# A chunked recurrence on TensorE: its triangular inverse multiplied into two operands ahead of the chain

## The chip, the cores and the metric

The kernel runs on one core of one Trainium2 chip. The metric is the device time of one execution in microseconds. TensorE is called PE, its weight loads PEld, VectorE DVE, ScalarE ACT, GpSimd POOL, and the queue that issues the DMAs SP.

## The reference

One inference step of a hybrid decoder layer, for 1024 new prompt positions and 8 sample rows: an input projection, a gated linear attention branch (GLA), an RWKV-7 branch, a gated merge of both, an output projection and a layer norm. What the change touches is the RWKV-7 branch, 16 heads of 64, whose recurrence the reference runs position by position:

```python
def _rwkv7_scan(r, w, k, v, kk, a, S0):
    def step(S, inp):
        rt, wt, kt, vt, kkt, at = inp
        sa = jnp.einsum('bhvk,bhk->bhv', S, -kkt)
        S = S * wt[:, :, None, :] + sa[..., None] * (kkt * at)[:, :, None, :] + vt[..., None] * kt[:, :, None, :]
        y = jnp.einsum('bhvk,bhk->bhv', S, rt)
        return S, y
...
p = jnp.einsum('btd,dn->btn', x, w_in)
r, kb, vb, g_b, w_lr, aa_lr = _split(pr, RWKV_SPLITS)
y, S_rwkv = _rwkv7_scan(rh, hr(w), kh, vh, kk, hr(a), S_rwkv0.astype(jnp.float32))
```

All is float32.

## The kernel before

The prompt is worked in two passes of 512 positions. In each pass the rows of the input projection (tile `proj` in PSUM, products of 128x128 weights with 256 to 512 columns, every one as three products of a high and a low part) are streamed through TensorE, and as soon as three rows of a pair of heads are there, a `pair` is started: eight pairs per pass, 16 in all, each with eight chunks of 64 positions. Beside them run the GLA heads and the gates; the up projections and the output projection come after.

Everything is written as generators that yield one operation at a time. A planner (`Order.run`) keeps an estimated time for each engine and each tile and issues, over all live generators, the operation that by its estimate can start first, with some preference by kind. So the program order of every engine is fixed when the kernel is built, and each engine runs its queue in that order. When the planner works out when an operation can start on TensorE (`start`), it adds a margin to the time at which another engine's result is ready: `SPARE`, 0.4 us for results of VectorE, ScalarE and GpSimd, and `LANDED`, 0.5, for a DMA. `self.C` is a copy that goes to ScalarE or VectorE, `self.E` an operation for VectorE or GpSimd, whichever ends first by the estimate.

A pair goes through these steps:

- `front` builds the scaled operands: `AZ` (the two left sides, 128 columns a chunk), `BK` and `GG`, the masked products within each chunk (`GG[:, x, 0]` for the chain's right side, `GG[:, x, 1]` for the output). Each chunk and head has a strictly triangular 64x64 matrix, whose unit triangular inverse is needed. Its diagonal 32x32 blocks go through DRAM (`LD`) into `L`, one block per partition, and are inverted into `X` by 31 steps on VectorE (a product into `Xt`, and an addition). The result goes back through DRAM (`XD`) into the tile `XT`, transposed, and into `X2`.
- `back` joins the two blocks of 32 into an inverse of 64: VectorE transposes the first block into `X1`, TensorE multiplies (`pA`), the result is copied (`A`), multiplied again (`pZ`), and copied into the off-diagonal part of `XT`.
- `turn` transposes `BK` on TensorE (into `bt`) and `v` (into `u`).
- `chain` runs the recurrence over the eight chunks, one pair after another: `pr` = `GG[:, x, 0]` with `u` (state and values stacked); copy to `rh`; `pu` = `XT[:, x]` with `rh`; copy the halves back to `u`; `pS` = `bt[:, x]` with `u`; and the next state from `pS`, into the next chunk's `u`. Each of the three products is 128x128 by 128 columns. After the chain, the outputs of all chunks come from two groups of products into `pY` and a `big` bank: 64x64 ones of `AZ` with the states, and 128x64 ones of `GG[:, x, 1, h]` with `u`.
- `norm` normalises, gates and writes the pair's rows.

[...] All operations are recorded by one line, L217, so that the groups in the profile are told apart by tiles. Instructions on float32 operands show as two records of TensorE each.

Of the kernel before, what the change touches and what calls it, by code (L numbers as in the profile page):

```python
# [20 lines left out]
P = 128  # L21
D = 1024
# [4 lines left out]
HT = TP // 2  # L27

PASS = [(0, HT + NS, NS, [(0, 256), (256, 264)]), (HT + NS, HT, 0, [(0, 512)])]
GH, GDK, GDV = 4, 128, 256  # L30
# [15 lines left out]
SBUF = {  # L46
    "row": ([P, HALF], 33), "wide": ([P, 2 * HT], 2), "bk": ([P, 3 * HT], 2), "gg": ([P, 4 * HT], 2), "lw": ([P, HT], 2),
    "l2s": ([P, 2 * P], 1), "pc": ([P, NCH], 3), "X": ([P, 256], 1),
    "Xt": ([P, P], 1), "L1": ([P, P], 1), "A": ([P, P], 1), "S": ([P, GDV], 2), "Sp": ([P, C], 2), "s0p": ([P, C], 2), "rh": ([P, P], 2),
    "sto": ([P, P], 1), "az": ([P, 2 * HT], 2), "bnd": ([P, 1], 3), "st": ([P, 32], 3), "part": ([P, HALF], 2), "l2p": ([P, 2 * P], 2),  # L50
    "pair": ([P, 2, HT // 32], 3), "nst": ([P, 2 * NCH], 2), "ac": ([P, HT // 4], 1),
}
# [19 lines left out]

AGE = 0.5

SPARE = 0.4
LANDED = 0.5
BIAS = 0.1
ASIDE = 0.5
# [162 lines left out]
def slow(op, us):  # L241

    op.lag = op.lag[0], op.lag[1] + us
    return op
# [11 lines left out]
class Order:  # L256
# [83 lines left out]
    def start(self, op):  # L340

        best = None
        for eng, fn, cost in op.ways:
            free, t = self.time[eng] + (SWITCH if eng == "P" and op.tiles != self.tiles else 0.0), 0.0
            for x in (*op.outs, *op.ins):
                at, by = self.ready.get(x.tensor.name, (0.0, None))
                if eng == "S" and by == "D" and x is op.out:
                    continue
                if by != eng:
                    at += HOP.get(by, 0.0) + (SPARE if eng == "P" and by in ("V", "A", "G") else LANDED if by == "D" else 0.0)  # L350
                elif eng != "P" and x is not op.out:
                    at += 0.13
                t = max(t, at)
            t = max(t, *(self.read.get(x.tensor.name, 0.0) for x in op.outs))
            if eng in op.port:
                free = max(free, self.port["G" if eng == "V" else "V"])
            late, t = free - t, max(t, free)
            if eng in "VA" and self.held(eng, op):
                cost += HOLD
            end = t + cost  # L360
            if len(op.ways) > 1:
                end += BIAS if eng == "V" and "A" in op.ways[0][0] else ASIDE if eng == "G" and "G" in op.port else 0.0
            if best is None or end < best[0]:
                best = end, t
                op.eng, op.fn, op.cost, op.late = eng, fn, cost, max(0.0, late)
        return best[1]
# [56 lines left out]
class Kern(Order):  # L423
# [711 lines left out]
    def front(self, c, p, st, d):  # L1135
# [85 lines left out]
        for q in range(4):  # L1221
            yield slow(self.S.dma_start(L_[NU * q:NU * q + NU], LD.rearrange("n c s t -> (n c) (s t)")), 1.0)
        tm = yield from self.get("Xt")
        for j in range(31):
            w, ni = 31 - j, j // 4 + 1
            tv = tm[:, :ni * w].rearrange("p (s t) -> p s t", t=w)
            yield V.tensor_mul(tv, X[:, 0:ni, j:j + 1].to_broadcast([P, ni, w]),
                               L[:, j:j + 1, j + 1:].to_broadcast([P, ni, w]))
            yield V.tensor_add(X[:, 0:ni, j + 1:], X[:, 0:ni, j + 1:], tv)
        self.free(tm)  # L1230
        XT = (yield from self.get("XT")).rearrange("p (c h t) -> p c h t", c=NCH, h=2)
        XD = self.dr.tile([4 * NCH, 32, 32], F32, name=f"XD{c.i}{p}")
        for q in range(4):
            yield slow(self.S.dma_start(XD.rearrange("u (i g) t -> g u i t", g=4)[q], X[NU * q:NU * q + NU]), 0.5)
        self.free(X_)

        L1 = (yield from self.get("L1")).rearrange("p (x t) -> p x t", t=32)
        X2 = (yield from self.get("X2")).rearrange("p (g t) -> p g t", t=P)
        H = NCH // 2
        for h in range(2):  # L1240
            for n in range(2):
                g = 2 * h + n
                yield slow(self.S.dma_start(L1[32 * g:32 * g + 32], GG[64 * h:64 * h + 32, H * n:H * n + H, 0, h, 32:64]), -0.5)
        for q in range(2):
            b = slice(32 * q, 32 * q + 32)
            for h in range(2):
                n = 2 * q + h
                yield self.S.dma_start(XT[HS[h]][b, :, h, b], XD[n * NCH:(n + 1) * NCH].rearrange("c s t -> s c t"))

        for x in range(H):  # L1250
            b = slice(32 * x, 32 * x + 32)
            yield self.S.dma_start(X2[b, :, b], XD[2 * NCH + x::H].rearrange("g s t -> s g t"))
        d.AZ, d.BK, d.G, d.XT, d.v, d.bonus, d.pc, d.L, d.L1, d.X2 = AZ, BK, GG, XT, st[2], st[1], pc, L_, L1, X2

    def back(self, d):
        GG, XT = d.G, d.XT

        H = NCH // 2
        X1 = (yield from self.get("X1")).rearrange("p (x t) -> p x t", t=P)
        q = [slice(32 * n, 32 * n + 32) for n in range(4)]  # L1260
        for h in range(2):
            for n in range(2):
                g = 2 * h + n
                yield self.V.transpose(X1[q[g], :, q[g]], XT[q[2 * h], H * n:H * n + H, h, 0:32])
        pA = yield from self.bank("big", [P, P])
        yield together([self.P.matmul(pA[q[x]], d.L1[:, x], X1[:, x], start=True, stop=True) for x in range(H)])
        A_ = yield from self.get("A")
        yield self.C.copy(A_, pA)
        self.free(pA, X1, d.L1)
        pZ = yield from self.bank("big", [P, H, 32])  # L1270
        yield together([self.P.matmul(pZ[q[g]], A_[:, q[g]], d.X2[:, g], start=True, stop=True) for g in range(4)])
        for h in range(2):
            for n in range(2):
                yield self.C.copy(XT[q[2 * h], H * n:H * n + H, h, 32:64], pZ[q[2 * h + n]])

        for h, hs in enumerate(HS):
            yield self.C.copy(GG[hs, :, 0, h], d.AZ[hs, :, 0])
        self.free(pZ, A_, d.X2)

    def turn(self, d):  # L1280

        bt = d.BK.rearrange("p c t -> p (c t)")[:, :2 * HT].rearrange("p (c h k) -> p c h k", c=NCH, h=2)
        pt = yield from self.get("big", 2)
        yield together([self.tr(pt[h][:, x * C:x * C + C], d.BK[hs, x, h * C:h * C + P])
                        for x in range(NCH) for h, hs in enumerate(HS)])
        for h in range(2):
            yield self.C.copy(bt[:, :, h], pt[h].rearrange("p (c k) -> p c k", k=C))
        self.free(*pt)
        d.bt = bt.rearrange("p c h k -> p c (h k)")
        d.u = d.L.rearrange("p (c h v) -> p c h v", c=NCH, h=2)  # L1290
        pt = yield from self.bank("big", [P, 4, P])
        for n in range(4):
            yield self.tr(pt[:, n], d.v[:, n * P:(n + 1) * P])
        self.free(d.v)
        for h in range(2):
            for n, hs in enumerate(HS):
                yield self.C.copy(d.u[HS[1 - h], n::2, h], pt[hs, :, h * C:h * C + C])
        self.free(pt)

    def chain(self, c, p, d):  # L1300
        A, V = self.A, self.V
        AZ, BK, GG, XT, pc = d.AZ, d.BK, d.G, d.XT, d.pc
        u_, bt_ = d.u, d.bt

        for h, hs in enumerate(HS):
# [7 lines left out]
        for x in range(NCH):  # L1313
            u = u_[:, x]
            pr = yield from self.bank("pch", [P, 2, C])
            yield self.P.matmul(pr, GG[:, x, 0], u, start=True, stop=True)
            rh = yield from self.get("rh")
            yield V.tensor_copy(rh, pr)
            self.free(pr)
            s0p = None  # L1320
            if x >= first:
                for h, hs in enumerate(HS):
                    yield A.copy(ss[hs, x], u[hs, h])
                s0p = yield from self.get("s0p")
                yield A.activation(s0p, ss[:, x], AF.Copy, scale=pc[:, x:x + 1])
            pu = yield from self.bank("pch", [P, 2, C])
            yield self.P.matmul(pu, XT[:, x], rh, start=True, stop=True)
            self.free(rh)
            for h, hs in enumerate(HS):
                yield self.C.copy(u[hs, h], pu[hs, h])  # L1330
            self.free(pu)
            pS = yield from self.bank("pch", [P, 2, C])
            yield self.P.matmul(pS, bt_[:, x], u, start=True, stop=True)
            for h, hs in enumerate(HS):
                un = u_[hs, x + 1, h] if x + 1 < NCH else S[hs]
                if s0p is None:
                    yield V.tensor_scalar(un, pS[hs, h], pc[hs, x:x + 1], None, ALU.mult)
                else:
                    yield V.scalar_tensor_tensor(un, pS[hs, h], pc[hs, x:x + 1], s0p[hs], ALU.mult, ALU.add)
            self.free(pS, *([] if s0p is None else [s0p]))  # L1340
# [10 lines left out]
            yield V.scalar_tensor_tensor(y[:, :, h], mean[:, :, h].unsqueeze(2).to_broadcast([P, H, C]), -1.0 / RN, pY[h],  # L1351
                                         ALU.mult, ALU.add)
        self.free(*pY, ss_)
        self.free(AZ, BK, u_, GG, XT, pc)
        if c.i:
            self.spawn(self.state(p, S), "state")
        else:
# [482 lines left out]
```

## Time and profile before

| | |
|---|---|
| median of 3 runs | 1489.15 us (1487.49 to 1490.96) |
| the profiled execution | 1487.92 us, span 1486.1 us |
| granted TensorE clock | 0.996 |
| busy, share of the span | PE 98%, PEld 85%, DVE 80%, ACT 58%, POOL 8% |
| DMA | 318.96 MB, 66.8% of 16 engines' span |
| the chain's products (`pch`) | from 135.2 us to 1262.1 us of the span |

In the rows of a profile, "out<-in" names the tiles without their numbers, then come the shapes and the count; "busy, mean" is a group's time and one record's; what stands behind the second bar is the idle time of the engine ahead of it and what ended it. In a timeline a row has its start, its length, the engine, the operation and the count of merged records. TensorE's records overlap each other, so that distances from start to start tell more than lengths.

### The profile page before, as it was taken

The numbers are of one execution on the slowest core, as the hardware profiler recorded it, in microseconds if no ns is written. First come the engines' busy times: TensorE is split into PE (matmuls) and PEld (weight loads), VectorE is DVE, ScalarE is ACT, GpSimd is POOL, SyncE is SP. The second block draws the span as 40 slices with busy tenths as digits, with TensorE's granted clock in tenths as the row PEclk, the third lists the DMA queues.
The fourth block names the chain that finished last, engine by engine and source line by source line (L and its number), as shares of the span: only waits on it lengthen the run. The fifth ranks groups of instructions, "written<-read, shape, count | busy, mean of one in ns | idle before, by whom it ended". The sixth has DMA issues, their size and how long they took to land. (4 is left out here: it accounts for less than half of the span.)

```text
span 1486.1 us, 31563 instructions
## 1 busy us (share of the span) xinstructions
PE 1449.8 (98%) x11158; PEld 1260.4 (85%) x11158; DVE 1194.8 (80%) x3255; ACT 857.7 (58%) x2196; POOL 113.6 (8%) x208
## 2 busy tenths in 40 slices
PE   9999999999999999999999999999999999999997
PEld 6998999899989998787777777878787898988786
DVE  6697889888998899879878989898877866755665
ACT  5666776676767776665754555474547645544210
POOL 1001010201010102000101020111001000000000
PEclk9999999999999999999999999999999999999999
DMA  8886786678676877566566556656564766888432
GB/s 299 273 285 202 250 296 214 226 253 295 202 258 211 294 229 258 170 224 188 160 198 179 155 190 191 192 154 188 174 189 138 229 210 221 295 293 271 139 107 85
DMA packets 211258, 318.96 MB, mean 215 GB/s; under 512 B 91811, under 2 KB 107180, under 8 KB 211100
## 3 DMA queue, kind: packets, MB, share of 16 engines
q1 hardware_dynamic: 211100, 316.93, 66.8%
q8 instruction: 89, 1.46, 0.4%
q14 instruction: 69, 0.57, 0.1%
HBM read 197.19 MB, written 118.61 MB: 212 GB/s over the span
## 5 line engine op out<-in xcount | busy, mean ns | idle before, releaser
L217 PE MATMUL proj<-xs,wpart 128*128 128x264 f32 (+2 forms) x5640 | 1017.7, 327 | 1.4 <-DVE row L217 0.8
L217 PEld LDWEIGHTS proj<-xs,wpart 128*128 128x128 f32 x5640 | 808.5, 189 | 80.3 <-issue 9.9
L217 ACT CAST wpart<-wraw 128x512 fp32r<-128x512 f32 x210 | 130.2, 623 | 103.5 <-PE proj L217 49.6
L217 DVE TENSOR_TENSOR row<-row 128x512 f32<-128x512 f32 (+7 forms) x321 | 166.3, 524 | 12.4 <-ACT row L217 5.6
L217 DVE TENSOR_TENSOR wpart<-wraw,wpart 128x512 fp32r<-128x512 f32 x207 | 145.2, 702 | 32.3 <-ACT wpart L217 31.4
L217 ACT ACTIVATE row<-row 128x512 f32<-128x512 f32 (+5 forms) x213 | 128.8, 610 | 14.4 <-DMA row<-sg 6.5
L217 POOL TENSOR_TENSOR row<-row 128x512 f32<-128x512 f32 (+5 forms) x64 | 72.7, 1143 | 746.3 <-DVE row L217 396.4
L217 DVE TENSOR_TENSOR Xt<-X,wide 128x60 f32<-128x60 f32 (+24 forms) x496 | 104.8, 211 | 11.7 <-DMA wide<-LD 1.8
L217 DVE TENSOR_TENSOR X<-X,Xt 128x60 f32<-128x60 f32 (+24 forms) x496 | 105.4, 213 | 10.0
L217 ACT ACTIVATE row<-proj,omu 128x256 f32<-128x256 f32 (+1 forms) x99 | 54.0, 546 | 93.5 <-PE proj L217 93.3
L217 PE MATMUL big<-xs,wpart 128*128 128x256 f32 (+2 forms) x576 | 101.7, 332 | 0.0
L217 PEld LDWEIGHTS big<-xs,wpart 128*128 128x128 f32 x576 | 87.7, 194 | 9.7 <-issue 0.2
L217 DVE SCALAR_TENSOR_TENSOR wide<-pch,pc,s0p 64x64 f32<-64x64 f32 x208 | 58.7, 282 | 32.9 <-PE pch L217 28.0
L217 ACT COPY row<-wide 64x64 f32<-64x64 f32 x240 | 57.9, 241 | 40.2 <-DVE wide L217 34.7
L401 ACT ACT_TABLE_LOAD x62 | 79.5, 1283 | 1.1
L217 DVE SCALAR_TENSOR_TENSOR row<-proj,pv,row 128x255 f32<-128x255 f32 (+1 forms) x99 | 56.3, 569 | 22.4 <-ACT tail L217 13.7
L217 PE MATMUL big<-row 128*32 128x32 f32 (+4 forms) x936 | 65.3, 241 | 1.4 <-ACT row L217 1.4
L217 ACT COPY row<-big 128x128 f32<-128x128 f32 (+6 forms) x134 | 38.7, 318 | 42.2 <-PE big L217 36.7
L217 ACT COPY wide<-pch 64x64 f32<-64x64 f32 x159 | 32.8, 206 | 47.0 <-PE pch L217 45.1
L217 ACT ACTIVATE row<-proj 128x128 f32<-128x128 f32 (+4 forms) x136 | 36.9, 324 | 37.4 <-PE proj L217 37.0
L217 PE MATMUL pch<-wide,gg 128*128 128x128 f32 x256 | 51.6, 283 | 5.5 <-DVE wide L217 4.7
L217 PEld LDWEIGHTS pch<-wide,gg 128*128 128x128 f32 x256 | 42.3, 189 | 16.1 <-PE proj L217 4.7
(249 smaller groups left out, 1992.6 us busy)
## 6 DMA issues: line engine op xcount, KB each, us to landing
w<-wpart SPq DMA_DIRECT2D x146, 512.0 KB
wpart<-w SPq DMA_DIRECT2D x146, 512.0 KB
wraw<-w_in SPq DMA_DIRECT2D x146, 256.0 KB
wide<-LD SPq DMA_DIRECT2D x64, 128.0 KB
wraw<-w_up_gla SPq DMA_DIRECT2D x32, 256.0 KB
wraw<-w_up_rwkv SPq DMA_DIRECT2D x32, 256.0 KB
sg<-row SPq DMA_DIRECT2D x16, 260.0 KB
row<-sg SPq DMA_DIRECT2D x16, 260.0 KB
```

What stands on the lines that cost most here:

```text
L217: ways.append((eng, lambda call=call: call(out, *args, **kw), price(eng, name, out, args, ins)))
L401: self.nc.scalar.preload_act_table_set(self.table)
```

## The change

The inverse is no longer applied in the chain to every chunk's right side. It is multiplied into `bt` and into the output matrix `GG[:, x, 1]` beforehand, in `turn`: with P the inverse, `bt`'·(P·r) becomes (P'-multiplied `bt`)'·r, and the same for the output. In the chain, `pr` is copied to `u` directly, and the product `pu` and the tile `rh` are gone: two products per chunk instead of three. To multiply in this order, the inverse is needed untransposed (`XI`, half as wide as `XT`): the solve runs over columns from the last to the first and reads `L` by columns, `X1` is loaded by DMA where `X2` was, and `back` transposes the other block and copies the quarters of `pA` into `X2`. The margin `SPARE` becomes one per engine: 0.6 for VectorE and GpSimd, 0.2 for ScalarE.

```diff
-SPARE = 0.4
+SPARE = {"V": 0.6, "G": 0.6, "A": 0.2}
...
-                    at += HOP.get(by, 0.0) + (SPARE if eng == "P" and by in ("V", "A", "G") else LANDED if by == "D" else 0.0)
+                    at += HOP.get(by, 0.0) + (SPARE[by] if eng == "P" and by in SPARE else LANDED if by == "D" else 0.0)
... (front)
-        for j in range(31):
-            w, ni = 31 - j, j // 4 + 1
-            tv = tm[:, :ni * w].rearrange("p (s t) -> p s t", t=w)
-            yield V.tensor_mul(tv, X[:, 0:ni, j:j + 1].to_broadcast([P, ni, w]),
-                               L[:, j:j + 1, j + 1:].to_broadcast([P, ni, w]))
-            yield V.tensor_add(X[:, 0:ni, j + 1:], X[:, 0:ni, j + 1:], tv)
+        LT = L.rearrange("p s t -> p t s")
+        for j in range(31, 0, -1):
+            i, ni = j // 4, 8 - j // 4
+            tv = tm[:, :ni * j].rearrange("p (s t) -> p s t", t=j)
+            yield V.tensor_mul(tv, X[:, i:, j:j + 1].to_broadcast([P, ni, j]),
+                               LT[:, j:j + 1, :j].to_broadcast([P, ni, j]))
+            yield V.tensor_add(X[:, i:, :j], X[:, i:, :j], tv)
...
-        XT = (yield from self.get("XT")).rearrange("p (c h t) -> p c h t", c=NCH, h=2)
+        XI = (yield from self.get("XT"))[:, :HT].rearrange("p (c t) -> p c t", c=NCH)
...
+        for h in range(2):
+            for n in range(2):
+                b, o = slice(64 * h + 32 * n, 64 * h + 32 * n + 32), h * NCH + H * n
+                yield self.S.dma_start(X1[b, :, b], XD[o:o + H].rearrange("c s t -> s c t"))
         for q in range(2):
             b = slice(32 * q, 32 * q + 32)
             for h in range(2):
                 n = 2 * q + h
-                yield self.S.dma_start(XT[HS[h]][b, :, h, b], XD[n * NCH:(n + 1) * NCH].rearrange("c s t -> s c t"))
+                yield self.S.dma_start(XI[HS[h]][b, :, b], XD[n * NCH:(n + 1) * NCH].rearrange("c s t -> s c t"))
-        for x in range(H):
-            b = slice(32 * x, 32 * x + 32)
-            yield self.S.dma_start(X2[b, :, b], XD[2 * NCH + x::H].rearrange("g s t -> s g t"))
... (back)
-                yield self.V.transpose(X1[q[g], :, q[g]], XT[q[2 * h], H * n:H * n + H, h, 0:32])
         pA = yield from self.bank("big", [P, P])
-        yield together([self.P.matmul(pA[q[x]], d.L1[:, x], X1[:, x], start=True, stop=True) for x in range(H)])
-        A_ = yield from self.get("A")
-        yield self.C.copy(A_, pA)
+        yield together([self.P.matmul(pA[q[x]], d.L1[:, x], d.X1[:, x], start=True, stop=True) for x in range(H)])
+        for x in range(H):
+            for h in range(2):
+                yield self.V.transpose(A_[q[x], 2 * h:2 * h + 2], XI[q[2 * h + 1], x::H, 32:64])
+        for x in range(H):
+            yield self.C.copy(X2[q[x], :, x], pA[q[x]].rearrange("p (g t) -> p g t", t=32))
... (turn)
+        pf = yield from self.get("big", 2)
+        pf = [y.rearrange("p (x k t) -> p x k t", k=2, t=C) for y in pf]
+        yield together([self.P.matmul(pf[h][HS[x % 2], x // 2, k], d.XI[hs, x], (bt[hs, x, h], d.G[hs, x, 1, h])[k], start=True, stop=True)
+                        for i in range(0, NCH, 2) for k in range(2) for x in (i, i + 1) for h, hs in enumerate(HS)], 0.5)
+        for k in range(2):
+            for h, hs in enumerate(HS):
+                for n in range(2):
+                    yield self.C.copy(d.G[hs, n::2, 1, h] if k else bt[hs, n::2, h], pf[h][HS[n], :, k])
+        self.free(*pf, d.XI)
... (chain)
             yield self.P.matmul(pr, GG[:, x, 0], u, start=True, stop=True)
-            rh = yield from self.get("rh")
-            yield V.tensor_copy(rh, pr)
-            self.free(pr)
...
-            pu = yield from self.bank("pch", [P, 2, C])
-            yield self.P.matmul(pu, XT[:, x], rh, start=True, stop=True)
-            self.free(rh)
             for h, hs in enumerate(HS):
-                yield self.C.copy(u[hs, h], pu[hs, h])
-            self.free(pu)
+                yield self.C.copy(u[hs, h], pr[hs, h])
+            self.free(pr)
```

More of the change, by code (lines that the diff above doesn't have):

```diff
@@ L48 @@
     "l2s": ([P, 2 * P], 1), "pc": ([P, NCH], 3), "X": ([P, 256], 1),
-    "Xt": ([P, P], 1), "L1": ([P, P], 1), "A": ([P, P], 1), "S": ([P, GDV], 2), "Sp": ([P, C], 2), "s0p": ([P, C], 2), "rh": ([P, P], 2),
+    "Xt": ([P, P], 1), "L1": ([P, P], 1), "A": ([P, P], 1), "S": ([P, GDV], 2), "Sp": ([P, C], 2), "s0p": ([P, C], 2),
     "sto": ([P, P], 1), "az": ([P, 2 * HT], 2), "bnd": ([P, 1], 3), "st": ([P, 32], 3), "part": ([P, HALF], 2), "l2p": ([P, 2 * P], 2),
@@ L1237, in front @@
         L1 = (yield from self.get("L1")).rearrange("p (x t) -> p x t", t=32)
-        X2 = (yield from self.get("X2")).rearrange("p (g t) -> p g t", t=P)
+        X1 = (yield from self.get("X1")).rearrange("p (x t) -> p x t", t=P)
         H = NCH // 2
@@ L1247, in front @@
                 n = 2 * q + h
-                yield self.S.dma_start(XT[HS[h]][b, :, h, b], XD[n * NCH:(n + 1) * NCH].rearrange("c s t -> s c t"))
-        for x in range(H):
-            b = slice(32 * x, 32 * x + 32)
-            yield self.S.dma_start(X2[b, :, b], XD[2 * NCH + x::H].rearrange("g s t -> s g t"))
[L1253 to L1260, printed above, removed]
+                yield self.S.dma_start(XI[HS[h]][b, :, b], XD[n * NCH:(n + 1) * NCH].rearrange("c s t -> s c t"))
@@ new lines, in front, with back @@
+        d.AZ, d.BK, d.G, d.XI, d.v, d.bonus, d.pc, d.L, d.L1, d.X1 = AZ, BK, GG, XI, st[2], st[1], pc, L_, L1, X1
+    def back(self, d):
+        GG, XI = d.G, d.XI
+        H = NCH // 2
+        q = [slice(32 * n, 32 * n + 32) for n in range(4)]
+        pA = yield from self.bank("big", [P, P])
+        yield together([self.P.matmul(pA[q[x]], d.L1[:, x], d.X1[:, x], start=True, stop=True) for x in range(H)])
+        A_ = (yield from self.get("A")).rearrange("p (g t) -> p g t", t=32)
+        for x in range(H):
+            for h in range(2):
+                yield self.V.transpose(A_[q[x], 2 * h:2 * h + 2], XI[q[2 * h + 1], x::H, 32:64])
+        X2 = (yield from self.get("X2")).rearrange("p (g x t) -> p g x t", g=4, t=32)
+        for x in range(H):
+            yield self.C.copy(X2[q[x], :, x], pA[q[x]].rearrange("p (g t) -> p g t", t=32))
+        self.free(pA, d.X1, d.L1)
+        pZ = yield from self.bank("big", [P, H, 32])
+        yield together([self.P.matmul(pZ[q[g]], A_[:, g], X2[:, g].rearrange("p x t -> p (x t)"), start=True, stop=True) for g in range(4)])
@@ L1261, in back @@
         for h in range(2):
             for n in range(2):
-                g = 2 * h + n
-                yield self.V.transpose(X1[q[g], :, q[g]], XT[q[2 * h], H * n:H * n + H, h, 0:32])
-        pA = yield from self.bank("big", [P, P])
-        yield together([self.P.matmul(pA[q[x]], d.L1[:, x], X1[:, x], start=True, stop=True) for x in range(H)])
-        A_ = yield from self.get("A")
-        yield self.C.copy(A_, pA)
-        self.free(pA, X1, d.L1)
-        pZ = yield from self.bank("big", [P, H, 32])
@@ L1271, in back @@
[L1271 to L1274, printed above, removed]
+                yield self.C.copy(XI[q[2 * h + 1], H * n:H * n + H, 0:32], pZ[q[2 * h + n]])
         for h, hs in enumerate(HS):
             yield self.C.copy(GG[hs, :, 0, h], d.AZ[hs, :, 0])
-        self.free(pZ, A_, d.X2)
+        self.free(pZ, A_, X2)
@@ L1298, in turn @@
         self.free(pt)
+        pf = yield from self.get("big", 2)
[7 more added lines that the diff above has]
+        self.free(*pf, d.XI)
     def chain(self, c, p, d):
         A, V = self.A, self.V
-        AZ, BK, GG, XT, pc = d.AZ, d.BK, d.G, d.XT, d.pc
+        AZ, BK, GG, pc = d.AZ, d.BK, d.G, d.pc
         u_, bt_ = d.u, d.bt
@@ L1353, in chain @@
         self.free(*pY, ss_)
-        self.free(AZ, BK, u_, GG, XT, pc)
+        self.free(AZ, BK, u_, GG, pc)
         if c.i:
```

## The prediction

> **What bounds the kernel now.** I read the page's busy table first, then its slices, then PE's own waits, and then single stretches of PE's timeline.
>
> ```profile
> span 1486.1 us, 31563 instructions
> PE 1449.8 (98%) x11158; PEld 1260.4 (85%) x11158; DVE 1194.8 (80%) x3255; ACT 857.7 (58%) x2196; POOL 113.6 (8%) x208
> PE   9999999999999999999999999999999999999997
> DVE  6697889888998899879878989898877866755665
> ```
>
> TensorE has work in every slice; the other engines have room, DVE least of all (eight or nine tenths through the middle). So a microsecond is gained by taking occupancy from PE's in-order queue or by taking out a wait at its head. What the waits come to, by PE's rows of the view of waits (engine, line, releaser: us in total, times, longest):
>
> ```profile
> PE pch L217 <- DVE wide L217: 6.0, 9, 1.7
> PE pch L217 <- DVE rh L217: 4.1, 4, 1.8
> PE big L217 <- DVE part L217: 3.0, 5, 0.9
> PE big L217 <- DVE row L217: 2.2, 3, 1.3
> PE big L217 <- DVE X L217: 1.7, 1, 1.7
> PE big L217 <- ACT row L217: 1.4, 2, 1.0
> PE big L217 <- DMA X<-XD: 1.2, 1, 1.2
> PE big L217 <- DVE S L217: 1.1, 3, 0.5
> PE pch L217 <- ACT wide L217: 1.0, 3, 0.5
> ```
>
> These are 21.7 us of the 36.3 us (1486.1 less 1449.8) in which PE is idle. The recurrence is not the bound: its links are issued between projection products, and PE is late for a link only in a few places. So the sum is one of PE occupancy, with a small term for waits.
>
> **Removed: one 128x128 product per chunk (`pu` from `XT` and `rh`), 2 passes x 8 pairs x 8 chunks = 128.** The page's group view says this, but the matmuls overlap there, so I take the price from the timeline, as what the product displaces among projection products:
>
> ```profile
> L217 PE MATMUL pch<-rh,XT 128*128 128x128 f32 x256 | 51.1, 281 | 4.1 <-DVE rh L217 4.1
> 603.54 0.38 PE L217 MATMUL pch<-rh,XT 128*128 128x128 f32 x2
> 603.68 1.63 PE L217 MATMUL proj<-xs,wpart 128*128 128x512 f32 x6
> 605.15 0.38 PE L217 MATMUL pch<-wide,bk 128*128 128x128 f32 x2
> ...
> 1298.22 16.82 PE L217 MATMUL big<-xs,wpart 128*128 128x512 f32 x72
> 1314.88 11.27 PE L217 MATMUL proj<-xs,wpart 128*128 128x512 f32 x48
> ```
>
> An undisturbed 128x512 product costs (1314.88 - 1298.22)/72 = 0.2314 us from start to start. From the `rh` product to the next link lie 605.15 - 603.54 = 1.61 us with six of those (1.39) in them: the f32 product, two records, costs 0.22 us. 128 x 0.22 = **28.2 us off PE**. Its busy time, 51.1 us, would be 0.40 each; I don't take it, because the tail of a record lies under the next one's head.
>
> **The wait for `rh` goes with it: 4.1 us** (row above), as the product that waited is gone. Late next is the same chunk's `u`: the copies from `pr` now come right behind `pr`, where they came behind `pu`; their wait (ACT wide, 1.0 us) is kept as it is. Nothing is queued behind a new wait in the chain: it has one hop through DVE and one link fewer.
>
> **Added in `turn`: 32 products of 64x64x64 per pair, 512 in all.** The profile has the same shape with the same order of quarters in the output block `pY` (row half by head, column half by chunk parity):
>
> ```profile
> 670.64 0.48 PE L217 MATMUL proj<-xs,wpart 128*128 128x512 f32 x1
> 671.05 0.27 PE L217 MATMUL pY<-row,az 64*64 64x64 f32 x1
> ...
> 671.16 0.22 PE L217 MATMUL pY<-row,az 64*64 64x64 f32 x1
> ...
> 671.45 0.22 PE L217 MATMUL pY<-row,az 64*64 64x64 f32 x1
> ...
> 671.51 0.22 PE L217 MATMUL big<-row,az 64*64 64x64 f32 x1
> 671.66 0.69 PE L217 MATMUL pY<-wide,gg 128*64 128x64 f32 x16
> ...
> 672.75 18.11 PE L217 MATMUL proj<-xs,wpart 128*128 128x512 f32 x77
> 690.78 0.41 PE L217 MATMUL big<-row 128*32 128x32 f32 x25
> ```
>
> From 671.16 to 671.45 five steps of four records pass, 0.058 us each; a step is two products (f32 is two records). 32 products are 16 steps: 0.93 us. The first step is 0.05 longer (671.05 to 671.16). Leaving for another shape takes 0.15 from the last record (671.51 to 671.66), 0.09 over a step. Entering from a projection takes 0.41 - 0.23 = 0.18. Returning costs something on the first projection: 690.78 - 672.75 = 18.03 against 77 x 0.2314 = 17.82, so at most 0.2 for this and the next change of shape; I take half, 0.1. A block is 0.93 + 0.05 + 0.09 + 0.18 + 0.10 = 1.35 us, 16 of them **21.6 us onto PE**. Bounds: 1.07 (17.1 in all) where entry and exit are shared with the transposes that `turn` has just issued; 1.45 (23.2) with the full 0.2. I take 1.35, as the nearest block in the trace stands among projections.
>
> **Copies and transposes on DVE and ACT.** Their groups, by shape:
>
> ```profile
> L217 DVE COPY rh<-pch 128x128 f32<-128x128 f32 x128 | 37.0, 289 | 17.5 <-PE pch L217 14.7
> L217 DVE COPY wide<-big 64x256 f32<-64x256 f32 x31 | 13.1, 423 | 4.7 <-PE big L217 4.2
> L217 ACT COPY wide<-big 64x256 f32<-64x256 f32 x33 | 12.1, 367 | 6.0 <-DVE wide L217 5.5
> L217 DVE STREAM_TRANSPOSE X<-XT 32x128 f32<-32x128 f32 x64 | 19.2, 300 | 4.9 <-DMA XT<-XD 4.3
> L217 ACT COPY XT<-big 32x128 f32<-32x128 f32 x43 | 11.0, 256 | 7.3 <-PE big L217 6.7
> ```
>
> Gone: 128 `rh` copies, 37.0 us of DVE. New: 8 copies of 64x256 out of `pf` per pair, 128 x 0.367 to 0.423 = 47 to 54 us over both engines. `back` has 128 half-sized transposes for 64 (each between half of 0.300 and all of it: 0 to 19 us more on DVE; nearer all, as fixed costs rule at this size, so 11) and four quarter copies for the one `A` copy (three more of 0.256, 12 us, mostly on ACT). Halved between the engines, DVE ends about even (-37 + 25 + 11 + 3) and ACT gains about 33 us on 857.7 of 1486.1. The cover is PE's projection work, which fills the queue while a pair is in `back` and `turn`; I cost it at nothing. Without the cover, the eight copies on two engines, 4 x 0.4 = 1.6 us per pair, would be waited for: 26 us.
>
> **The rest, in one go.** The solve counts down instead of up; its pairs of instructions keep their number and sizes (31 to 1 columns by 1 to 8 blocks), and only L is read down a column. The DMAs keep their number and shape: four loads into `X1` for the four into `X2`, ahead of the four into `XI` on SP's queue, so `XI` comes four issues later and the first product in `back` now waits for `X1`'s landing in place of DVE's transposes (the 1.7 us wait `<- DVE X` becomes one for a DMA like the 1.2 us one): nothing, between -1.7 and +1.2. `XT`'s buffer is free before the chain instead of after it, and the new need of two `big` banks lasts some 3 us per pair.
>
> **Margins.** The order is planned with 0.6 us in hand for DVE and POOL results at PE (0.4 before) and 0.2 for ACT's. The 20 DVE waits in the rows that remain (9 + 5 + 3 + 3) lose at most 0.2 us each, 4.0 us; the five ACT waits gain 0.2 each, 1.0 us, and others can appear. I take **-2.0**, between -4.0 and a loss that I price as a rival.
>
> **Sum**: -28.2 + 21.6 - 4.1 - 2.0 = -12.7 us. The profiled execution took 1487.92 us (span 1486.1 and 1.8 around it), so 1475.2; it lay 1.2 us under the median of 1489.15, to which I add it: **1476 us**. What counts as no change is 0.2%, 3 us.
>
> **The rivals.**
>
> *Slower: ACT's results come too late at PE.* With 0.2 us less in hand, each product fed by ACT may stall PE 0.2 us. There are some 430 such places:
>
> ```profile
> L217 ACT CAST wpart<-wraw 128x512 fp32r<-128x512 f32 x210 | 130.2, 623 | 103.5 <-PE proj L217 49.6
> L217 ACT COPY wide<-pch 64x64 f32<-64x64 f32 x159 | 32.8, 206 | 47.0 <-PE pch L217 45.1
> ```
>
> and 64 casts of `xs`. Without the -2.0 the sum is -10.7; it turns into a loss over 3 us when 13.7 us are stalled, 69 places, one in six. At one in four, 108 x 0.2 = 21.6, the time is 1489 - 10.7 + 21.6 = 1500. Against it: ACT stands still 103.5 us ahead of the casts alone, and PE has only five such waits in the rows above. 0.12.
>
> *No change: the gain goes into new waits.* `pf` must be copied before the chain starts, and DVE is the fullest of the helpers. If half of the 26 us of copies shows at PE, 1476 + 13 = 1489. For it: DVE's eights and nines; against it: 21.7 us of waits in 1486. 0.09.
>
> *More gained: the shorter chain also ends the waits on `wide`, and blocks share their switches.* 6.0 us of `<- DVE wide` and 21.6 - 17.1 = 4.5 more, with the full 4.0 of the margins: 1476 - 6.0 - 4.5 = 1465.5, and with the overlap of the first two taken as none, some 1464. For it: `turn` issues its transposes just ahead; against it: `u` still comes over the same DVE hop from `pS`. 0.14.
>
> *The solve slows down.* In column order an element lies 128 bytes from the next. If each paid its time twice, then by the groups kept apart by shape (for `pc`, the view of its tile: min/median/max)
>
> ```profile
> L217 DVE TENSOR_TENSOR Xt<-X,wide 128x76 f32<-128x76 f32 x16 | 3.9, 244 | 0.3
> L217 DVE TENSOR_TENSOR Xt<-X,wide 128x24 f32<-128x24 f32 x16 | 3.0, 186 | 0.4
> L217 DVE COPY pc<-row x15: 156/164/664, 55.2 to 1144.2; 128x8 f32<-128x8 f32 x15
> L217 DVE TENSOR_SCALAR nkk<-pv 128x8 f32<-128x8 f32 x1 | 0.2, 165 | 0.0
> ```
>
> (244 - 186)/52 = 1.1 ns an element, 1560 elements per pair and 16 pairs, 27 us of DVE; all of it at PE would make 1503. Against it: `pc` takes eight elements 260 bytes apart in a median 164 ns, and `nkk` eight adjacent ones in 165. 0.03. [...]
>
> *Four quarters don't run side by side in `pf`*: 16 steps become 32, 0.93 us more a block, +15: 1491. `pY` speaks against it, 0.02.
>
> **How the numbers follow.** 0.60 for 1476 (its own range 1468 to 1484, from blocks of 1.07 to 1.45 us and margins of -4 to +2), 0.14, 0.09, 0.12, 0.03, 0.02 for the others in the order more, none, ACT, solve, quarters. Faster by over 0.2%: 0.60 + 0.14 and a little of "none", 0.76; within: 0.10; slower: 0.14. From 1463 to 1491 lies all but the two slow ends and the lower part of "more", under 0.2.
>
> **What the changed profile would show.** 256 `pch` product records in each of two groups, none from `rh`; a group of 1024 64x64 records into `big` with 0.058 us steps; PE's waits at 15 to 20 us with fewer `<- DVE` and a few more `<- ACT`; DVE's busy time within 15 us of 1194.8 and ACT's some 30 higher; the `Xt<-X,wide` means as they were. I am wrong if the blocks cost over 1.8 us, or if PE's idle time grows past 45 us.

## The result, and the profile after

| | before | after |
|---|---|---|
| median | 1488.32 us (1485.46 to 1490.96, 4 runs) | 1501.61 us (1498.94 to 1504.05, 4 runs) |
| profiled execution, span | 1486.1 us | 1502.3 us |
| granted TensorE clock | 0.996 | 0.988 |

The ratio is 1.0091, with a 95% interval of 1.0068 to 1.0114: the kernel became slower by 13 us, where 1476 us was forecast. The page of the changed kernel, its busy table and two rows of its slices:

```profile
span 1502.3 us, 33264 instructions
PE 1452.7 (97%) x11926; PEld 1254.1 (83%) x11926; DVE 1212.1 (81%) x3207; ACT 894.2 (60%) x2335; POOL 117.4 (8%) x223
PE   9999999999999999999999999999999989999997
PEclk9999999999999999999999999999999999999999
```

PE is idle for 1502.3 - 1452.7 = 49.6 us, 13.3 more than before, and its busy time has not fallen. The slices hide why: nine tenths of the clock and full clock print the same digit. The mean granted clock shows it. If PE's pace follows the clock, as it does in the block of products below (1.09 us at full clock, 2.11 at half), (1 - 0.988) x 1502.3 = 18.0 us were lost to a reduced clock, against (1 - 0.996) x 1486.1 = 5.9 before, 12.1 more. Nearly all of that lies within PE's busy time (some 2 us of it in each kernel fall behind the last product). What PE does at full clock fell from 1449.8 - 5.9 = 1443.9 to 1452.7 - 18.0 = 1434.7. So the 16.2 us between the two profiles are 13.3 of idle time, 12.1 of clock, and -9.2 of work. (The clock is given to three digits; each clock term is good to some 0.8 us.) This split belongs to one execution, the slowest of the four: the other three of the changed kernel had granted clocks of 0.992, 0.989 and 0.994, which by the same sum are 12.0, 16.5 and 9.0 us lost.

At this place the forecast has 28.2 off and 21.6 on, -6.6 us. The -9.2 us bears that out only roughly, because PE's busy time holds more than the products' own work: two runs below, `n1_order` and `r6_rows`, have the same products in the same order and granted clocks of 0.996 and 0.995, and yet 5.3 us between their busy times:

```profile
PE 1441.8 (97%) x11926; PEld 1246.8 (84%) x11926; DVE 1217.4 (82%) x3247; ACT 876.1 (59%) x2287; POOL 121.9 (8%) x227
PE 1436.5 (97%) x11926; PEld 1247.9 (84%) x11926; DVE 1202.1 (81%) x3247; ACT 873.4 (59%) x2287; POOL 122.4 (8%) x227
```

What the new products cost is better read from PE's timeline. One block of them:

```profile
656.16 1.08 PE L217 MATMUL proj<-xs,wpart 128*128 128x512 f32 x4
657.18 0.34 PE L217 MATMUL big<-bk,XT 64*64 64x64 f32 x8
657.34 0.30 PE L217 MATMUL big<-gg,XT 64*64 64x64 f32 x8
657.46 0.30 PE L217 MATMUL big<-bk,XT 64*64 64x64 f32 x8
...
658.04 0.30 PE L217 MATMUL big<-gg,XT 64*64 64x64 f32 x8
658.27 1.66 PE L217 MATMUL proj<-xs,wpart 128*128 128x512 f32 x6
```

From 657.34 to 657.46 eight records (four products, one for each head and chunk parity) pass in 0.12 us, so a step of four takes 0.058 as in `pY`. The block lasts from 657.18 to 658.27, 1.09 us, with 0.10 of entry in front of it (1.02 for four projections of 0.2314). With the slow first projection behind it that is the 1.35 us of the forecast, within 0.1. In the trace 15 of the 16 blocks last 1.09 us from their first product to the next one behind them; the last, at half clock, lasts 2.11.

PE's waits, in the view of waits of the changed kernel:

```profile
PE big L217 <- DMA X<-XD: 6.0, 3, 3.0
PE big L217 <- DMA XT<-XD: 5.6, 7, 1.2
PE pch L217 <- DVE wide L217: 4.7, 10, 0.9
PE big L217 <- DVE part L217: 3.7, 3, 2.3
PE big L217 <- ACT X L217: 3.3, 1, 3.3
PE big L217 <- DVE X L217: 2.7, 2, 1.8
PE proj L217 <- DMA wpart<-w: 2.3, 1, 2.3
```

The wait for `rh` is gone, as said. At the top stand 11.6 us for the inverse's blocks coming out of `XD`; before, this was 1.2. Ten times PE stood in front of the first product of `back` until the loads had landed; the profile puts these down to `X` or `XT`, which are issued one behind the other. The longest of these on PE's timeline:

```profile
487.83 2.41 PE L217 MATMUL proj<-xs,wpart 128*128 128x264 f32 x19
493.25 0.47 PE L217 MATMUL big<-X,L 128*32 128x128 f32 x8 [3.01 <-DMA X<-XD]
493.65 4.36 PE L217 MATMUL proj<-xs,wpart 128*128 128x256 f32 x22
```

And what such a wait does to the clock, by stretches of the changed kernel (length; busy time of PE, PEld, DVE, ACT, POOL with counts; granted clock; DMA):

```profile
262.00:264.80 2.80, 0.52 (x4) 0.34 (x3) 2.80 (x6) 1.36 (x3) 1.89 (x6) 1.00 0.61 143
264.80:268.20 3.40, 3.40 (x20) 2.86 (x21) 2.88 (x7) 1.44 (x3) 0.00 (x0) 0.50 0.67 176
299.50:302.40 2.90, 1.13 (x9) 0.92 (x9) 2.74 (x8) 0.00 (x0) 1.10 (x2) 0.99 0.53 215
302.40:305.80 3.40, 3.40 (x16) 3.12 (x15) 3.01 (x11) 2.04 (x10) 0.00 (x0) 0.50 0.07 27
490.50:493.50 3.00, 0.25 (x8) 0.19 (x8) 1.77 (x3) 1.35 (x3) 0.86 (x4) 1.00 0.61 148
493.50:496.90 3.40, 3.40 (x23) 3.25 (x16) 2.62 (x10) 0.71 (x4) 0.00 (x0) 0.50 0.94 312
497.00:520.00 23.00, 23.00 (x272) 21.10 (x271) 17.02 (x33) 17.77 (x55) 3.83 (x7) 1.00 0.76 261
```

Behind 3.00 us in which PE is busy for 0.25, the clock is at half for 3.4 us. If PE does half as much in them, as the block of 2.11 us against 1.09 says, the wait of 3.0 us costs some 1.7 more, an estimate (half of 3.4). The first pair of stretches shows the same behind a wait for `part`, the second behind 1.8 us of idle time (2.90 less 1.13). The kernel before has this too, behind several waits close together near its end (2.3 us of idle time in 4.30), but not behind 1.8 us of idle time at 781 us:

```profile
781.00:784.00 3.00, 1.17 (x6) 0.69 (x6) 2.97 (x8) 0.61 (x1) 0.00 (x0) 1.00 0.32 119
784.00:787.00 3.00, 3.00 (x16) 2.24 (x14) 2.87 (x8) 1.45 (x4) 0.00 (x0) 1.00 0.29 71
1232.00:1236.30 4.30, 2.01 (x14) 1.60 (x13) 4.24 (x10) 3.67 (x9) 0.00 (x0) 1.00 0.58 223
1236.30:1243.00 6.70, 6.18 (x30) 5.98 (x29) 2.54 (x7) 3.04 (x8) 0.00 (x0) 0.50 0.66 197
```

So the length of a wait does not decide alone; what decides beside it, no run shows. In the trace's clock records all half-clock stretches of the changed kernel begin whole multiples of 3.41 us apart: those at 264.8, 302.4, 493.5, 592.5 and 988.4 us lie 11, 56, 29 and 116 such steps from one to the next. That 1.8 to 3.0 us of standing still were enough at these places is measured; that they are enough everywhere is not, by the 1.8 us at 781.

Last, the solve. All its products and those of 8 elements in the kernel before, then the same groups as in the forecast in the changed kernel:

```profile
L217 DVE TENSOR_TENSOR Xt<-X,wide 128x60 f32<-128x60 f32 (+24 forms) x496 | 104.8, 211 | 11.7 <-DMA wide<-LD 1.8
L217 DVE TENSOR_TENSOR Xt<-X,wide 128x8 f32<-128x8 f32 x16 | 2.6, 162 | 0.2
...
L217 DVE TENSOR_TENSOR Xt<-X,wide 128x60 f32<-128x60 f32 (+24 forms) x496 | 127.1, 256 | 14.4 <-DMA wide<-LD 4.2
L217 DVE TENSOR_TENSOR Xt<-X,wide 128x76 f32<-128x76 f32 x16 | 4.7, 294 | 0.4
L217 DVE TENSOR_TENSOR Xt<-X,wide 128x24 f32<-128x24 f32 x16 | 2.9, 182 | 0.3
L217 DVE TENSOR_TENSOR Xt<-X,wide 128x8 f32<-128x8 f32 x16 | 2.6, 164 | 0.3
```

127.1 us where the page before has 104.8: 22 us more on VectorE, 1.4 us per pair. At 8 and at 24 elements nothing is lost (164 ns after 162, 182 after 186), but these take one and three elements of a column of L, each for eight blocks; between 24 and 76 (19 of a column for four blocks) each further element costs (294 - 182)/52 = 2.2 ns where it cost (244 - 186)/52 = 1.1. The planner's price for these products is by their size alone, so it takes every result of the solve, and what follows it on VectorE, as ready earlier than it is.

### The profile page after: what moved, and what is told of

The parts are those of the page before. It is cut to its first block, busy times and chain, and to the rows that moved or that the text cites. A ratio compares the mean times of both kernels' runs of the same rounds, so it can differ in the third digit from the quotient of the medians.

```text
span 1502.3 us, 33264 instructions
## 1 busy us (share of the span) xinstructions
PE 1452.7 (97%) x11926; PEld 1254.1 (83%) x11926; DVE 1212.1 (81%) x3207; ACT 894.2 (60%) x2335; POOL 117.4 (8%) x223
## 4 chain that ended last, share of the span: by engine, by line
PE 68%; DVE 18%; DMA 6%; SPq 3%; issue 3%; ACT 2%; POOL 0%; POOLq 0%; DVEq 0%; ACTq 0%
PE proj L217 40%; PE big L217 21%; DVE row L217 6%; SPq L217 3%; PE pY L217 3%; PE pch L217 3%; DVE Xt L217 3%; DVE X L217 3%; DVE wpart L217 1%; ACT row L217 1%; DMA wpart<-w 1%; DVE wide L217 1%; DMA wide<-LD 1%; DVE pair L217 1%; DMA X<-XD 1%
## 5 line engine op out<-in xcount | busy, mean ns | idle before, releaser
L217 DVE TENSOR_TENSOR row<-row 128x512 f32<-128x512 f32 (+8 forms) x328 | 170.1, 526 | 8.0 <-ACT row L217 3.2
L217 DVE TENSOR_TENSOR wpart<-wraw,wpart 128x512 fp32r<-128x512 f32 x199 | 138.5, 698 | 30.6 <-ACT wpart L217 29.3
L217 DVE TENSOR_TENSOR Xt<-X,wide 128x60 f32<-128x60 f32 (+24 forms) x496 | 127.1, 256 | 14.4 <-DMA wide<-LD 4.2
L217 DVE TENSOR_TENSOR X<-X,Xt 128x60 f32<-128x60 f32 (+24 forms) x496 | 110.0, 222 | 9.8
L217 POOL TENSOR_TENSOR row<-row 128x512 f32<-128x512 f32 (+5 forms) x57 | 62.7, 1103 | 638.8 <-DVE row L217 257.9
L217 PE MATMUL big<-xs,wpart 128*128 128x512 f32 (+2 forms) x576 | 100.2, 330 | 0.3 <-DVE xs L217 0.2
L217 PEld LDWEIGHTS big<-xs,wpart 128*128 128x128 f32 x576 | 86.4, 191 | 10.8 <-DVE xs L217 0.8
L217 ACT COPY row<-wide 64x64 f32<-64x64 f32 x240 | 58.0, 242 | 60.3 <-DVE wide L217 51.1
L217 ACT COPY row<-big 128x128 f32<-128x128 f32 (+6 forms) x157 | 43.3, 301 | 64.1 <-PE big L217 43.2
L217 ACT CAST xs<-row 128x520 fp32r<-128x520 f32 (+1 forms) x64 | 38.5, 623 | 29.4 <-PE big L217 11.7
```

The costliest lines, as they stand in the source:

```text
L217: ways.append((eng, lambda call=call: call(out, *args, **kw), price(eng, name, out, args, ins)))
```

## The experiments

Two theories stood first: that the inverse comes too late (by the column reads and by X1's landing), and that the margins put PE ahead of its results. "Bias" below is a constant of the planner, `ASIDE`, that counts against giving an operation to GpSimd; changing it makes another order of the same work, with some operations on other engines.

**Margins undone; margins alone.** `SPARE` at 0.4 for all in the changed kernel, and the new dictionary in the kernel before.

> The changed kernel with the margin of before (0.4 us for each engine). Theory 1 (late inverse: reading L by columns makes the solve longer than the planner's price, so PE stands at the first product of back until X1 has landed, and long stalls halve PE's clock): the margin is no part of it, the time stays at 1496 to 1506 us, with over 8 us of PE waits for DMAs out of XD. Theory 2 (the margins put PE ahead of its results): it falls to 1480 or less.

> The kernel before with the new margins alone (0.6 us for VectorE and GpSimd, 0.2 for ScalarE). Theory 1: within 4 us of before, as nothing of the inverse changes. Theory 2: 1495 or more, with over 6 us of PE waits on ScalarE where before had 3.5.

The first took 1497.36 us (ratio to before 1.0066, 1.0046 to 1.0085), the second 1486.15 (0.9997, 0.9982 to 1.0012). The margins alone change nothing that can be measured; the forecast took -2.0. Theory 2 fell with these two: in the kernel before, PE's waits for ScalarE were 3.6 us with the new margins and 3.5 without. In the changed kernel they are 6.9 us in seven places, and 3.4 with the margins undone; that is far from the 21.6 us of the forecast's slower rival, but the 4 us by which the first run is below the changed kernel are not told apart from another order (see below). Theory 1 missed one of its signs in that run: the waits for `XD` were 6.7 us, under the 8 expected.

**L read along its rows.** The same instructions in the same order on every engine, with other addresses; the inverse is then not the right one.

```diff
-                               LT[:, j:j + 1, :j].to_broadcast([P, ni, j]))
+                               L[:, j:j + 1, :j].to_broadcast([P, ni, j]))
```

> The changed kernel, but the solve reads L along its rows (contiguous) where it should read columns, so the inverse is not the right one; the order of all instructions is the same as in the changed kernel. Theory 1: the products into Xt fall back from 127 us to about 105, PE's waits for DMAs out of XD from 11.6 us to under 6, fewer clock halvings, and the time to 1488 or less. Theory 2: 1498 to 1504 as the changed kernel. A third theory (the copies of pf load DVE and ACT): also 1498 to 1504.

1488.15 us (1.0008, 0.9995 to 1.0022): 13.5 us less than the changed kernel. The group `Xt` is back:

```profile
L217 DVE TENSOR_TENSOR Xt<-X,wide 128x60 f32<-128x60 f32 (+24 forms) x496 | 108.0, 218 | 14.2 <-DMA wide<-LD 3.9 <-issue 0.2
```

But theory 1 was wrong about the way: the waits for `XD` should have fallen under 6 us, and its waits are

```profile
PE big L217 <- DMA XT<-XD: 4.3, 6, 1.1
PE big L217 <- DMA X<-XD: 3.5, 2, 2.8
```

7.8. What fell was PE's idle time, from 49.6 to 43.0 us, and the stretches at half clock, from seven (30.7 us) to three (13.7), which is 8.5 us of the gain. So what the column reads cost does not come through the waits for `XD` alone. The third theory, that the copies of `pf` cost the time, expected 1498 or more and fell here too.

**Both prices of the planner mended; X1's landing alone.** `e5_priced` adds 0.7 ns per element to the price of the column-read products and 1.5 us to the landing time of X1's loads; `e4_x1_late` only the latter:

```diff
-                yield self.S.dma_start(X1[b, :, b], XD[o:o + H].rearrange("c s t -> s c t"))
+                yield slow(self.S.dma_start(X1[b, :, b], XD[o:o + H].rearrange("c s t -> s c t")), 1.5)
```

> The changed kernel with two prices of the planner mended and nothing else: 0.7 ns more per element for the solve's column-read products, and 1.5 us later landing for the loads of X1. Theory 1: PE waits for DMAs out of XD fall under 3 us, PE's clock is halved in at most four places, and the time comes to 1476 to 1488. Theory 2: no change beyond the noise of the order, 1495 or more.

> The changed kernel with X1's loads planned 1.5 us later, the solve's price left as it is. If the wait at X1's landing was the larger part of what the priced version gained: 1490 to 1494, with no PE wait for DMAs out of XD. If it was the price of the column reads (all of VectorE's results were planned too early): 1496 or more, although those waits are gone.

1491.62 us (1.0040, 1.0028 to 1.0053), and 1483.50 (0.9970, 0.9955 to 0.9986). In the second, the waits for `XD` are down from 11.6 to 1.1 us:

```profile
PE big L217 <- DMA X<-XD: 0.6, 1, 0.6
PE big L217 <- DMA XT<-XD: 0.5, 1, 0.5
```

Both came out of their ranges: the priced one worse than expected, with no `XD` wait left, and the half-mended one better than it. A planner with the truer price lost to one with the falser: the first sign that the order as such moves the time by as much as the causes do.

**Both causes away; another way round; another order.** `e6_rows_x1_late` joins the two edits above. `e7_copied` lets ScalarE turn L within each partition, and keeps the later landing of X1:

```diff
+        two = yield from self.rows(2, 512)
+        LT = [x.rearrange("p (t s) -> p t s", s=32) for x in two]
+        for q in range(2):
+            yield A.copy(LT[q], L[:, :, 16 * q:16 * q + 16].rearrange("p s t -> p t s"))
```

> The solve reading L along rows (so the inverse is not the right one) and X1's loads planned 1.5 us later. If column reads and X1's landing are two causes that add up, and they are all that stood between the changed kernel and the sum of its products: PE idle 33 to 38 us, at most three halvings of the clock, and 1474 to 1482 us. If something else costs the rest (the copies of pf, or the order itself): 1484 to 1490.

> The changed kernel computing the right thing with the column reads taken from VectorE: ScalarE copies L transposed within each partition into two free row buffers, and the solve reads that along rows; X1's loads planned 1.5 us later. ScalarE gets 16 x 2 copies of 512 elements, some 20 to 35 us. If the column reads and X1's landing were the causes: 1476 to 1486. If the order as such or the copies of pf are: 1488 or more.

> [...] Each theory that names a cause expects 1496 to 1507; a time under 1492 would say that the slowdown was an accident of this one order.

1471.52 us (0.9890, 0.9870 to 0.9909), 1497.61 (1.0065, 1.0034 to 1.0096) and 1489.29 (1.0009, 0.9995 to 1.0023). The first is below its range, and below the sum that the forecast made; its partner in the same order is `e4_x1_late`, 12.0 us above it. The second removes the column reads from VectorE (`Xt` at a median of 212 ns) and is slow all the same, with 10.1 us of waits for `part` in ten places and five stretches at half clock. It is no clean trial of the column reads, as the solve now waits for ScalarE's copies:

```profile
L217 DVE TENSOR_TENSOR Xt<-X,row 128x60 f32<-128x60 f32 (+24 forms) x496 | 110.5, 223 | 29.9 <-ACT row L217 19.5
```

The third, with `ASIDE` at 0.6 in place of 0.5, moved 12 us by an edit that means nothing, to under the 1492 that was to speak for an accident of one order. From here on, a single order proved nothing, and each version was taken in three.

> The changed kernel in a third order (bias against GpSimd 0.4 in place of 0.5; 0.6 gave 1489). If the changed kernel's 1501.6 is one end of a spread of orders: anything from 1485 to 1504, most likely 1488 to 1498. PE waits of 8 us or more for DMAs out of XD in any case.

> The same third order's bias, with X1's loads planned 1.5 us later. If the wait at X1's landing costs by itself, whatever the order: 5 to 18 us under the run without (its partner in this set), at 1478 to 1488. If the gain at the bias of 0.5 was an accident of that order: within 5 us of its partner on either side.

> The bias of 0.6 with X1's loads planned 1.5 us later; without, 0.6 gave 1489.3. If the landing costs by itself: 1477 to 1485. If not: 1486 to 1495.

> The kernel before, planned with a bias of 0.6. If orders scatter by some 5 us on this kernel as on any: 1480 to 1493. If the kernel before was planned in a lucky order: over 1493, and then part of the changed kernel's loss is the luck of the kernel before.

> The same with a bias of 0.4: 1480 to 1493, or over 1493 by the second reading.

> The changed kernel at a bias of 0.6 (1489.3) in the same order of instructions, the solve reading L along rows (the inverse is not the right one). If the column reads cost what they cost at 0.5 (13.5 us): 1474 to 1479. If their price at 0.5 was due to the halvings of the clock in that order: 1482 to 1488.

> The changed kernel at a bias of 0.4 (1487.1) in the same order, rows read likewise. 1472 to 1477 by the first reading, 1480 to 1486 by the second.

**A version that needs neither column reads nor X1 by DMA.** It solves by rows as before, loads `A` from `XD` and turns the other blocks over on VectorE:

```diff
+                yield self.V.transpose(X1[q[2 * h + n], :, q[2 * h + n]], XB[q[2 * h], H * n:H * n + H, 0:32])
...
+                yield self.V.transpose(XI[q[2 * h + n], :, 32 * n:32 * n + 32], XB[q[2 * h + n], :, 32 * n:32 * n + 32])
...
-                yield self.V.transpose(A_[q[x], 2 * h:2 * h + 2], XI[q[2 * h + 1], x::H, 32:64])
```

> The changed kernel with the solve of before (rows of L, giving the transposed inverse): the lower block is then loaded by DMA into A, the upper one and the diagonal of XI are turned over by VectorE (4 transposes of 32x128 and 4 of 32x256 per pair, in place of 8 of 32x64), and X1 comes from VectorE as before, so that neither column reads nor a wait of PE for X1's landing are left; it computes the right thing. VectorE: 22 us less in the solve, 30 less for A's transposes, 19 and some 28 more for the new ones. If the two named causes are right: 1472 to 1484 us. If only the order decides: 1484 to 1500.

> The version that turns the blocks over on VectorE, with the bias at 0.6. It took 1477.3 at 0.5. If it is better by what it leaves out and not by its order: 1472 to 1484. If by its order: 1485 or more.

> The same at a bias of 0.4: 1472 to 1484, or 1485 or more by the second reading.

All medians in us, by the planner's bias. Each set of runs was timed beside the kernel before, whose median was 1486.45 to 1488.32 us from set to set, so differences between sets are good to 1 or 2 us.

| | 0.4 | 0.5 | 0.6 | mean |
|---|---|---|---|---|
| before | 1485.76 | 1486.84 | 1495.37 | 1489.3 |
| after | 1487.14 | 1501.61 | 1489.29 | 1492.7 |
| after, L read along rows (same orders as "after") | 1477.23 | 1488.15 | 1481.24 | 1482.2 |
| after, X1's landing 1.5 us later | 1485.20 | 1483.50 | 1480.42 | 1483.0 |
| after, L along rows and X1's landing later | | 1471.52 | | |
| after, blocks turned over on VectorE | 1492.79 | 1477.32 | 1486.26 | 1485.5 |

What follows, row by row:

- *The order alone* moves the kernel before by 9.6 us and the changed one by 14.5. The changed kernel as timed is the slowest of its three; the kernel before, as timed, is not (its 1495.37 is over the 1493 that was to show a lucky order, its 1485.76 is not). On the means over three orders the change costs 3 us, not 13, and three orders don't tell 3 from nothing. What sets the slow order apart is not its waits for `XD`, which are alike in the three (11.6, 9.5 and 10.6 us): PE is idle for 49.6 us there and for 43.4 and 42.5 in the other two, at granted clocks of 0.988 against 0.996 and 0.996.
- *Column reads* cost 13.5, 8.1, 9.9 and, with X1's landing later, 12.0 us, in four pairs that have the same order of instructions. By the ratios to the kernel before in the same set it is 12, 6, 10 and 12. This is shown; how it reaches PE is not. At 0.6 and 0.4 the waits for `XD` stay (9.5 and 8.6 us; 10.6 and 10.8), and both times fell between the two ranges expected.
- *X1's landing*: the waits go away in all three (at most 1.1 us with the later landing), and the times are 18.1, 8.9 and 1.9 us lower. The sign is the same three times, but 1.9 us was to mean an accident of the order by what was expected; the size isn't told apart from that of the order, which changes along with it.
- *The change without its column reads* is 7 us below before on the means, where the sum of the products said 6.6 and the whole sum 12.7; with its waits for `XD` still in it, that this lies so near to 6.6 proves little.
- *The turned-over version* at 1477.32 us (0.9938, 0.9918 to 0.9959) is the fastest that does the whole computation, and beats both kernels; but in two other orders it took 1486.26 (0.9994, 0.9980 to 1.0007) and 1492.79 (1.0043, 1.0026 to 1.0061). By what was expected of these two, it is faster at 0.5 by its order. In the slow one the long waits are for the low part of a split:

```profile
PE big L217 <- DVE part L217: 13.7, 7, 9.0
```

The more solid gain is the later landing of X1: below before in all three orders, by 0.6 to 15 us against the same bias, and clear of the timed kernel before at 0.5 and 0.6 (there 0.9961, 0.9947 to 0.9975), but not at 0.4 (0.9991, 0.9974 to 1.0008).

## Why the prediction was wrong, point by point

- **Removed products and added products**: right in kind, and the new block in size (1.09 us and its switches, against 1.35). The total, -9.2 us of busy time at full clock against -6.6, agrees only as far as busy time is work. Distances from start to start in the timeline carried this; the groups' busy column would have said something else (51.1 us gone, and 17.6 + 16.9 come).
- **The solve "keeps its number and sizes", at no cost**: the step that failed first. It cost 22 us on VectorE and 13.5 us of the time in this order (6 to 12 in the others). The rival was there with the right place and nearly the right price on VectorE (27 us), but with a chance of 0.03 from a row that could not decide: eight elements of `pc` at 260 bytes. The changed kernel's own row for eight elements shows nothing either (164 ns, before 162), while 76 elements take 294 against 244: from 24 to 76 an element costs twice (2.2 ns against 1.1), as the rival had it, and up to 24 no more than before (182 ns against 186). That the rival's 1503 lies next to the measured 1501.61 is luck: it put all 27 us at PE, where the column reads are 13.5 of the 25.6 us between forecast and result. `Xt`'s mean, which the forecast expected unchanged, went from 211 to 256 ns.
- **"The first product in `back` now waits for `X1`'s landing": nothing, between -1.7 and +1.2**: it waited 11.6 us. Before, VectorE stood at that landing (4.3 us in its row for the transposes, off the path); the change moves the wait to PE's queue, where projections stand behind it (4.36 us of them behind the wait of 3.01 in the timeline above). What this cost in time is not shown, as no run takes it out in the same order. The forecast named the move, and priced it by a row of another load that is read later.
- **The margins, -2.0**: nothing measurable (0.9997). The slower rival by ScalarE's results, priced at 21.6 us, wasn't it either: PE waits 6.9 us for ScalarE in all. (In the rival "more gained", the 4.0 us of the margins are named but are not in the 1465.5; with them it is 1463.5.)
- **The clock** has no term in the sum, and the page before had its sign: 0.996, with the clock at half from 1236.3 us on, behind 2.3 us of idle time in 4.30. 12.1 of the 16.2 us between the profiles are clock. A wait of 3.0 us with the clock at half for 3.4 us behind it is dearer than its length, by the estimate above some 1.7 us.
- **The scatter of orders**: the range of 1463 to 1491 took the planner's order as if it were given. An edit that changes prices or operations re-deals all of it, and that is worth 10 to 15 us by itself.
- **The copies and transposes at nothing**: VectorE 1212.1 less the 22 of the solve is 1190 (forecast: about even), ScalarE +36.5 (33); the 128 half-sized transposes took 237 ns each where the 64 of before took 300, 11.1 us more (11). They were not taken out by themselves in a run, so that they are covered is supported by these sums and not shown.
- **What was to show it wrong**: "PE's idle time past 45 us"; it is 49.6.

What stays open: why a given order makes the few long waits; how VectorE's 22 us become 6 to 13 at PE; and how much of the 18 us by which X1's later landing helps at the bias of 0.5 is the landing itself.

## What to carry to other kernels

Where a program's order comes from a planner, an edit is timed together with a new order: take both kernels in three meaningless variations of it before believing a per cent. Where an edit keeps sizes but changes strides, read the price from instructions of several lengths with that stride, the longest above all, or pay for a kernel that differs in the addresses alone, which keeps the order. And when a wait moves from a helper to the engine that bounds the kernel, price it there, with the clock that it loses behind it.

## What the runs showed of the hardware that was not expected

- VectorE took longer to read float32 128 bytes apart, 294 ns against 244 in adjacent ones at 76 elements, but not in the instructions that take one or three elements of a column: nothing that can be seen at 8 and 24 elements (164 ns against 162, 182 against 186). From 24 to 76 it is 2.2 ns for each further element against 1.1.
- ScalarE took longer too. Its copies in `e7_copied`, which turned L on it by reads 128 bytes apart, beside a copy of as many elements per partition in runs of 64 adjacent ones:

```profile
L217 ACT COPY row<-wide 128x512 f32<-128x512 f32 x32 | 35.5, 1142 | 4.6 <-DMA wide<-LD 3.9 <-DMA row<-OS 0.7
L217 ACT COPY bk<-bk 64x512 f32<-64x512 f32 x16 | 9.9, 617 | 5.9 <-DVE bk L217 5.6
```

1142 ns against 617, 1.03 ns more per element, in copies that differ also in their partitions (128 and 64).
- In the changed kernel TensorE's clock was at half for 3.4 us behind 1.8 to 3.0 us of waiting, and such stretches began whole multiples of 3.41 us apart, as shown above; in the kernel before it stayed full behind 1.8 us.
